# A transformer's opening laid out anew: the order of its first loads, silu of c from a broadcast load, own buffers for ten modulation loads

## The chip, the cores and the metric

The kernel runs on one core of a Trainium2 chip. The metric is the device time of one execution in microseconds (us); less is better. A core has TensorE (PE; its weight loads are listed as PEld), VectorE (DVE), ScalarE (ACT), GpSimd (POOL) and SyncE (SP), which issues all of this kernel's DMAs on one queue.

## The reference, cut to what matters

Two transformer blocks over 256 tokens of width 1024, in float32. The first block has two layers; each is modulated by a vector `c`:

```python
mod = jax.nn.silu(c) @ ada_w + ada_b
sh_m, sc_m, gt_m, sh_f, sc_f, gt_f = jnp.split(mod[:, None, :], 6, axis=-1)
h = rms_norm(x, norm_mix) * (1 + sc_m) + sh_m
(aq, ak, av, ..., cqkv, cz, ca, cb) = jnp.split(h @ w_in, points, axis=-1)
# window attention, sparse attention, gated delta rule -> o_a, o_b, o_c
x = x + gt_m * (jnp.concatenate([o_a, o_b, o_c], axis=-1) @ w_out)
h = rms_norm(x, norm_ffn) * (1 + sc_f) + sh_f
gate, up = jnp.split(h @ w_gate_up, 2, axis=-1)
x = x + gt_f * ((jax.nn.silu(gate) * up) @ w_down)
```

The second block has a cross attention to a memory `mem_2` of 256 rows of width 1024. Its keys and values are `rms_norm(mem_2, mem_norm_2) @ cross_wk_2` and `... @ cross_wv_2`. They depend on nothing else, and so they can be worked out first.

## The kernel before, in words

Features lie on the 128 partitions in eight blocks, tokens along the free axis. All weights are packed into one DRAM array in chunks of 128 rows by 1024 columns (512 KB; the token chunks `("win", l, "tok", i)` have 1104). A float32 product is made of three matmuls on parts: `weight` (L386) fetches a chunk into a `raw` buffer (L364; four of them), ACT copies it into a rounded high part `hi` (L393), VectorE subtracts to the low part `lo` (L394), and `mm3` (L425) multiplies hi by hi, hi by lo and lo by hi. The subtraction is the last reader of `raw`. A full chunk takes 24 matmuls for 256 tokens.

The modulation is not done on TensorE. `ada` (L668) fetches one column block of `ada_w` (512 KB) into a `side` buffer (four of them), and VectorE multiplies it by silu(c), which stands along the free axis of every partition (`crow`), and sums (L672). `ada_spread` (L410) sets how many columns are worked out beside each weight; `weight` counts that up and calls `ada` behind the split:

```python
        self.ada_due += self.ada_rate
        while self.ada_due >= 1 and self.ada_jobs:
            self.ada(*self.ada_jobs.pop(0))
            self.order(self.ada_last, d)
            self.ada_due -= 1
```

`order` fixes the order of two instructions of one engine, so that VectorE runs split, columns, next split. In the same way all loads are issued by SP in the order of the program (`load_last`, L364 and L649). Within what is fixed, a scheduler orders the instructions and gives buffers to tiles by a forecast of its own, at compile time; it adds a wait where a tile takes over a buffer.

The opening is `setup` (L633), `ada_spread` of 16 columns over `ADA0 = 11` weights and `mem_keys` (L1379), called in `run` (L1697). `setup` loads c as a column, the early column constants (`colt`: gains, biases), the memory in four loads (`mem_load`, L1368) and two constants (identity, ones). `mem_keys` then calls `c_row` (L660): 16 matmuls that turn silu(c) from a column into rows, and two copies out of PSUM. Next it scales the memory by its gain in two parts (`mem_parts`, L1374), and works out the memory's statistics: squares (ACT), sums (VectorE, PE), `rstd` (L441: VectorE, then a power on POOL), and `spread_sb` (L715: matmuls and a copy), which gives 1/rms along the free axis (`R`). Then come the keys: for each pair of eight weights wk0 to wk7 two times 24 matmuls (`ws`, L565) and a product with R into `memk` (L1398); behind the first and the second pair, two loads of x each. Then the values wv3 to wv7 (`mem_values`, L1402), with transposes.

In `run` the first layer follows: modulation bias (`ada_bias`), squares of x, `norm_hT` (L558), which for each of eight feature blocks makes a product on VectorE (L530), a high part on ACT (L535) and a low part on VectorE (L536), and `mixer` (L787). The mixer's steps are traced in the order of the string `SEQ[l]` (L271): `0` to `3` are heads of the delta rule, whose first step multiplies the chunk `("win", 0, ("qkv", 0), 0)`, `t` the token chunks (`tokens`, L797, `tok_steps`, L586). The chunks of layer 1's tokens are split ahead at the end of layer 0 (L1732).

Of the kernel before, what the change touches and what calls it, by code (L numbers as in the profile page):

```python
# [19 lines left out]
L = 2  # L20
# [5 lines left out]
CHUNK_COLS = 1104  # L26
# [27 lines left out]

def _plan():
# [3 lines left out]
    for l in range(L):  # L59
        for j in range(48):  # L60
            p["ada", l, j] = j
        for g, cols in WIN.items():
            for i, ks in enumerate(([0, 1, 2, 3], [4, 5, 6, 7]) if len(cols) > 128 else (K8,)):
                p["win", l, g, i] = [("w_in", l, ks, cols)]
# [154 lines left out]
def _pack(inputs):  # L219
# [26 lines left out]
    for l in range(L):  # L246
# [8 lines left out]
        "ccol": np.ascontiguousarray(i["c"].reshape(8, 128).T),  # L255
# [13 lines left out]
# the order in which the steps of a mixer are traced: 0..3 heads of the delta rule, i j inverses and x y outputs of its pairs,  # L269
# t tokens and decay, L loads, A modulation, c compress, r rope, m compressed, a window, b selected, z gate, p project, v memory values  # L270
SEQ = {0: "0tLttt0t001L11L1201i2ii22i3iiii32i3iAi3ii3jjjjcjijxcjjxjjcjjjxcxcjyycrcyrArrAAAyrrAArrmrabbAaaaabbbmbbbbAbbbzzAAzzAAzzApppAApApApAApAAAA",  # L271
       1: "vttvtv0vtt0001110211i2iiiiiii2333ii33iii2ixxxcc2jcjjjjjjjjjrjxcjjcjcrryrrrryyayacrrbmmbaAbaAAAbAbAzAbabAbzzbbbzzbzppppppp"}
HELD, HELD2 = 9, 8

# [6 lines left out]
def run(a):  # L281
    """traces a generator to its end and returns what that returns"""
    while True:
        try:
            next(a)
        except StopIteration as e:
            return e.value


def merge(a, b):  # L290
    """traces two generators in turns"""
    live = [a, b]
    while live:
        for g in list(live):
            if next(g, live) is live:
                live.remove(g)


class Net:
    def __init__(self, tc, ins, out):  # L300
# [6 lines left out]
        self.hold, self.held = (None, None), 0  # L307

# [55 lines left out]
    def fetch(self, key, tag="raw", bufs=4):  # L364
        off, n, _ = PLAN[key]
        cols = CHUNK_COLS if tag == "raw" else 1024
        raw = self.raw.tile([128, cols], F32, tag=tag, name=self.name("raw"), bufs=bufs)
# [8 lines left out]
    def order(self, later, earlier):  # L376
        """issue order of two instructions of one engine"""
# [3 lines left out]
    def ahead(self, keys):  # L381
        """weights that are loaded and split before they are asked for"""
        for k in keys:
            self.pre[k] = self.weight(k)

    def weight(self, key):  # L386
# [16 lines left out]
        self.ada_due += self.ada_rate  # L403
# [6 lines left out]
    def ada_spread(self, jobs, weights):  # L410
        """modulation columns to be worked out beside the next weights"""
# [3 lines left out]
    def pe(self, d):  # L415
        """keeps the tensor engine in the order of the trace while self.pe_order is set"""
# [29 lines left out]
    def row_rstd(self, halves, outs):  # L446
        """1 over the root mean square of the rows whose parts of 512 are given; outs are overwritten"""
# [18 lines left out]
    def to_hT(self, xn, scale, hi, lo, kcs):  # L466
        """xn: token tiles; hi(kc), lo(kc) [128, 256]: features on partitions, scaled, in two parts"""
# [12 lines left out]
    def square(self, b, gain=None, x=None):  # L480
        """feature blocks 2b and 2b+1 of (x * gain) ** 2, in addends of their sum"""
# [9 lines left out]
    def sums(self, sq, soon=False, after=None):  # L491
        """sums over features, tokens on partitions: PSUM [128, 2]"""
# [21 lines left out]
    def spread(self, r):  # L514
        """one value per token, along the free axis of all partitions: PSUM [128, 256]"""
# [10 lines left out]
    def norm_block(self, m, R, scale, shift, hi, lo):  # L526
        """x * scale * R (+ shift) in two parts, feature block m"""
# [10 lines left out]
    def scaled(self, m, scale, hi, lo, x=None):  # L538
        """x * scale in two parts, feature block m"""
# [5 lines left out]
    def new_hT(self, shift=None):  # L545
        """features on partitions, two parts; with shift, two more columns that hold it"""
# [6 lines left out]
    def pairs(self, n=4):  # L553
        """the same in pieces of two feature blocks"""
# [10 lines left out]
    def ws(self, keys, hT, turns=False, p=None):  # L565
        """features on partitions: [128, len(keys), 256] in one bank; turns: one feature block of hT after the other"""
# [19 lines left out]
    def tok_steps(self, keys, hT, outs):  # L586
        """tokens on partitions: outs[t] [128, n]; the chunks split the contraction"""
        n = 8 // len(keys)
        for i, key in enumerate(keys):
            wh, wl = (a.rearrange("p (k c) -> p k c", k=n) for a in self.weight(key))  # L590
            for t in range(2):
                ts = slice(t * 128, t * 128 + 128)
                for k in range(n):
                    kc = n * i + k
                    self.mm3(outs[t], (hT[0](kc)[:, ts], hT[1](kc)[:, ts]), (wh[:, k], wl[:, k]), kc == 0, kc == 7)
            yield
# [4 lines left out]
    def into(self, accs, m, l, w, first, last):  # L601
        """output features of block m: += w.T @ l; the two blocks of a bank form one accumulation group"""
# [13 lines left out]
    def project_steps(self, name, l, oT, accs, after=(), late=2, turn=range(8)):  # L616
        """1024 output features on partitions; the last contraction blocks finish one bank after the other"""
# [14 lines left out]
    # ------------------------------------------------------------------  # L632
    def setup(self):  # L633
# [7 lines left out]
        self.ccol = self.fix.tile([128, 8], F32, name="ccol")  # L641
        nc.vector.memset(self.mhalf, -0.5)
        self.loads([(self.ccol, ins["ccol"]), (self.colt[:, :COLS_EARLY], ins["cols"][:, :COLS_EARLY])])
        self.mem = self.mem_load()
        self.load_consts("ident", "one")
        nc.scalar.activation(self.ccol, self.ccol, AF.Silu)
# [13 lines left out]
    def c_row(self):  # L660
        """silu(c) along the free axis of all partitions"""
        for h in range(2):
            p = self.ps()
            for i in range(4):
                self.mm(p[:, i * 128:i * 128 + 128], self.ccol[:, 4 * h + i:4 * h + i + 1].to_broadcast([128, 128]), self.cc("ident"))
# [1153 lines left out]
```

## Time and profile before

| what | value |
|---|---|
| median of 3 runs | 1382.38 us |
| the three runs | 1381.71, 1382.38, 1386.05 us |
| span of the profiled execution, first to last instruction | 1381.5 us |
| mean granted TensorE clock of the profiled execution | 0.990 |
| PE, DVE, ACT, POOL busy, share of the span | 97%, 72%, 52%, 3% |
| moved by DMA | 276.71 MB, mean 200 GB/s |

The profile lists no other time of the profiled execution than its span; it lies 0.2 us under the fastest of the three runs. Busy time of PE is not PE at its peak, as its matmuls are pipelined and their ends are modelled. Where a line of the kernel is a helper (L393, L394, L423), the tile names tell the stages apart: `oT` holds the memory in two parts during the opening, `psw` is the bank that chunks accumulate into, `hhi` and `hlo` are the normed x.

### The profile page before, as it was taken

The page shows a single profiled execution, that of the slowest core. Times are in us where ns is not written, and L with a number is a line of the kernel's source. Part 1 is how long each engine was busy: PE and PEld are TensorE (multiplying, and loading weights), DVE is VectorE, ACT ScalarE, POOL GpSimd, SP SyncE. Part 2 cuts the span into 40 slices and gives each one's busy share as a digit, 9 for nine tenths or more (in the row PEclk, how much of TensorE's full clock was granted, in tenths as well). Part 3 has the DMA queues.
Part 4 walks back from the last instruction along what each step waited for, and adds up shares of the span by engine and source line. Part 5 has one row for each costly group of instructions (what it writes and reads, how often), then busy time and mean ns, then how long its engine had stood idle before and what let it go on. Part 6 is the DMA issues. An engine that isn't in the chain of part 4 may idle for free.

```text
span 1381.5 us, 26414 instructions
## 1 busy us (share of the span) xinstructions
PE 1341.2 (97%) x10632; PEld 1280.3 (93%) x10632; DVE 990.2 (72%) x1869; ACT 721.1 (52%) x1353; POOL 44.8 (3%) x55
## 2 busy tenths in 40 slices
PE   5899999999999999999999999999999999999998
PEld 5799879899999997889999999999987999999998
DVE  6888688998886886768666676665576664755554
ACT  4495274654445753666444454444456754644442
POOL 2001000000000010000000000000000000000000
PEclk9999999999999999999999999999999999999999
DMA  8974638899985445235666545555554563455551
GB/s 293 315 270 145 229 124 292 307 352 326 306 289 163 159 153 212 87 136 181 218 208 205 199 138 188 185 187 188 188 184 141 164 207 121 159 187 188 188 184 48
DMA packets 78747, 276.71 MB, mean 200 GB/s; under 512 B 9120, under 2 KB 9888, under 8 KB 78624
## 3 DMA queue, kind: packets, MB, share of 16 engines
q1 hardware_dynamic: 78624, 275.02, 58.7%
q8 instruction: 83, 1.36, 0.4%
q14 instruction: 40, 0.33, 0.1%
HBM read 271.31 MB, written 3.15 MB: 199 GB/s over the span
## 4 chain that ended last, share of the span: by engine, by line
PE 71%; issue 15%; DVE 7%; ACT 3%; DMA 2%; POOL 1%; SPq 0%; POOLq 0%; DVEq 0%; ACTq 0%
PE psw L423 41%; PE psb L423 22%; PE psi L423 5%; DVE lo L394 2%; PE psb L431 2%; DMA raw<-in_wbig_dram 1%; PE psb L1100 1%; ACT hi L393 1%; DVE raw L672 1%; POOL trs L444 1%; DVE hlo L543 1%; DVE xres L697 1%; POOL rr L943 1%; DMA xres<-in_x_dram 1%; DVE conv L921 0%
## 5 line engine op out<-in xcount | busy, mean ns | idle before, releaser
L394 DVE TENSOR_TENSOR lo<-raw,hi 128x1024 fp32r<-128x1024 f32 (+1 forms) x390 | 474.8, 1222 | 115.5 <-ACT hi L393 54.5
L423 PE MATMUL psw<-hhi,hi 128*128 128x256 f32 (+1 forms) x1744 | 496.6, 285 | 3.6 <-ACT hi L393 2.6
L423 PE MATMUL psw<-hhi,lo 128*128 128x256 f32 (+1 forms) x1744 | 494.9, 284 | 0.5 <-DVE lo L394 0.5
L423 PE MATMUL psw<-hlo,hi 128*128 128x256 f32 (+1 forms) x1744 | 495.1, 284 | 0.2 <-DVE hlo L543 0.2
L393 ACT ACTIVATE hi<-raw 128x1024 fp32r<-128x1024 f32 (+1 forms) x390 | 398.5, 1052 | 129.0 <-PE psw L423 66.4
L423 PEld LDWEIGHTS psw<-hhi,hi 128*128 128x128 f32 x1744 | 330.8, 190 | 5.9 <-ACT hi L393 3.2
L423 PEld LDWEIGHTS psw<-hlo,hi 128*128 128x128 f32 x1744 | 331.8, 190 | 1.6 <-issue 0.8
L423 PEld LDWEIGHTS psw<-hhi,lo 128*128 128x128 f32 x1744 | 331.8, 190 | 1.4 <-DVE lo L394 1.0
L423 PE MATMUL psb<-flo,hi 128*128 128x256 f32 x704 | 196.5, 281 | 0.0
L423 PE MATMUL psb<-fhi,lo 128*128 128x256 f32 x704 | 196.5, 281 | 0.0
L423 PE MATMUL psb<-fhi,hi 128*128 128x256 f32 x704 | 194.1, 281 | 0.2
L423 PEld LDWEIGHTS psb<-flo,hi 128*128 128x128 f32 x704 | 132.5, 188 | 0.2
L423 PEld LDWEIGHTS psb<-fhi,lo 128*128 128x128 f32 x704 | 132.5, 188 | 0.0
L423 PEld LDWEIGHTS psb<-fhi,hi 128*128 128x128 f32 x704 | 131.0, 188 | 1.0 <-ACT fhi L463 1.0
L672 DVE CUSTOM_DVE_ANT_0 raw<-raw,constt 128x1024 f32<-128x1024 f32 x96 | 116.0, 1218 | 0.0
L743 ACT ACTIVATE fa<-gu 128x256 f32<-128x256 f32 x44 | 18.4, 418 | 154.9 <-DVE gu L736 154.9
L423 PE MATMUL psb<-oT,hi 128*128 128x256 f32 x512 | 92.8, 283 | 0.0
L463 ACT ACTIVATE fhi<-fa 128x256 fp32r<-128x256 f32 x88 | 36.7, 418 | 97.6 <-DVE fa L741 54.9
L736 DVE TENSOR_TENSOR gu<-psw,R 128x512 f32<-128x512 f32 x44 | 30.4, 692 | 70.0 <-PE psw L423 66.5
L423 PEld LDWEIGHTS psb<-oT,hi 128*128 128x128 f32 x512 | 78.9, 188 | 0.3
L733 DVE TENSOR_TENSOR gu<-psw,R 128x256 f32<-128x256 f32 x88 | 37.0, 423 | 55.6 <-PE psw L423 53.6
L423 PE MATMUL psb<-oT,lo 128*128 128x256 f32 x256 | 71.8, 281 | 0.0
(368 smaller groups left out, 1753.9 us busy)
## 6 DMA issues: line engine op xcount, KB each, us to landing
raw<-in_wbig_dram SPq DMA_DIRECT2D x498, 512.0 KB, 4.4
raw<-in_wbig_dram SPq DMA_DIRECT2D x4, 552.0 KB, 5.6
mem<-in_mem_dram SPq DMA_DIRECT2D x8, 256.0 KB, 6.9
xres<-in_x_dram SPq DMA_DIRECT2D x4, 256.0 KB, 7.1
memd<-memk SPq DMA_DIRECT2D x4, 256.0 KB, 7.4
mk<-memd SPq DMA_DIRECT2D x4, 256.0 KB, 5.2
mv<-memd SPq DMA_DIRECT2D x2, 512.0 KB, 7.2
out_dram<-out SPq DMA_DIRECT2D x4, 256.0 KB, 2.4
```

The lines of the kernel that those rows point to most:

```text
L393: a = self.nc.scalar.activation(hi[:, :n], r, AF.Copy)
L394: d = self.nc.vector.tensor_tensor(lo[:, :n], r, hi[:, :n].bitcast(F32), op=OP.subtract)
L423: return self.pe(self.nc.tensor.matmul(out, lhsT, rhs, start=start, stop=stop))
L431: self.pe(self.nc.tensor.transpose(out, in_, self.cc("ident")))
L444: self.nc.gpsimd.tensor_tensor(dst, dst, self.mhalf[:, :n], op=OP.pow)
L463: self.nc.scalar.activation(hi, src, AF.Copy)
L543: self.nc.vector.scalar_tensor_tensor(lo(m), x, s, hi(m).bitcast(F32), op0=OP.mult, op1=OP.subtract))
L672: self.ada_last = self.nc.vector.tensor_tensor_reduce(w, w, self.crow, 1.0, 0.0, OP.mult, OP.add, m[:, j:j + 1])
L697: v.scalar_tensor_tensor(self.xk(m), a, gate[:, m:m + 1], self.xk(m), op0=OP.mult, op1=OP.add)
L733: nc.vector.tensor_tensor(s[:, i * 256:i * 256 + 256], p[i][:, :256], R, op=OP.mult)
L736: nc.vector.tensor_tensor(s.rearrange("p (a t) -> p a t", a=2), p.rearrange("p (a t) -> p a t", a=2), self.b3(R, 2), op=OP.mult)
L743: nc.scalar.activation(a, p[:, :256], AF.Silu)
```

## The change

- The opening's loads come in another order: the memory's gain by itself (4 KB, `memg`), the memory in two loads, wk0, wk1, c, the early column constants, identity and ones; then wk2 and the rest. x is loaded behind the second and third pair of weights, not behind the first and second.
- c is loaded along the free axis of all partitions with one broadcast load (128 times 4 KB), and one ACT instruction makes silu of it; `ccol`, the 16 matmuls and two copies go.
- wk0 and wk1 are fetched and split ahead of the pair's matmuls, and count no modulation columns: the 16 columns then lie beside the eleven weights wk2 to wv7.
- The first ten modulation loads have buffers of their own (`OWN = 10`), the rest share the four as before.
- The memory's statistics are traced behind the first pair's matmuls.
- The token chunks of both layers are three (3, 3 and 2 feature blocks; 828, 828 and 552 columns) instead of two of 1104, and the weight buffers are 1024 columns wide instead of 1104; one more `t` stands in each `SEQ`. What is split ahead for layer 1 stays two chunks.

```diff
-CHUNK_COLS = 1104
+CHUNK_COLS = 1024
...
+KCS = {"tok": ([0, 1, 2], [3, 4, 5], [6, 7]), True: ([0, 1, 2, 3], [4, 5, 6, 7]), False: (list(range(8)),)}
...
-            for i, ks in enumerate(([0, 1, 2, 3], [4, 5, 6, 7]) if len(cols) > 128 else (K8,)):
+            for i, ks in enumerate(KCS[g if g == "tok" else len(cols) > 128]):
...
-SEQ = {0: "0tLttt0t001L11L12...
+SEQ = {0: "0tLtttt0t001L11L12...
-       1: "vttvtv0vtt00011...
+       1: "vtttvtv0vtt00011...
+OWN = 10
...
     def fetch(self, key, tag="raw", bufs=4):
-        raw = self.raw.tile([128, cols], F32, tag=tag, name=self.name("raw"), bufs=bufs)
+        if tag == "side" and self.own:
+            self.own -= 1
+            raw = self.g4("own")
+        else:
+            raw = self.raw.tile([128, cols], F32, tag=tag, name=self.name("raw"), bufs=bufs)
...
-    def weight(self, key):
+    def weight(self, key, beside=True):
...
-        self.ada_due += self.ada_rate
+        self.ada_due += self.ada_rate if beside else 0
...
     def tok_steps(self, keys, hT, outs):
-        n = 8 // len(keys)
-        for i, key in enumerate(keys):
+        first = 0
+        for key in keys:
+            n = PLAN[key][1] // outs[0].shape[1]
...
-                    kc = n * i + k
+                    kc = first + k
...
     def setup(self):
-        self.ccol = self.fix.tile([128, 8], F32, name="ccol")
+        self.memg = self.fix.tile([128, 8], F32, name="memg")
         nc.vector.memset(self.mhalf, -0.5)
-        self.loads([(self.ccol, ins["ccol"]), (self.colt[:, :COLS_EARLY], ins["cols"][:, :COLS_EARLY])])
+        o, n = COLS.at["mem_norm_2"]
+        self.loads([(self.memg, ins["cols"][:, o:o + n])])
         self.mem = self.mem_load()
-        self.load_consts("ident", "one")
-        nc.scalar.activation(self.ccol, self.ccol, AF.Silu)
...
     def c_row(self):
-        for h in range(2):
-            p = self.ps()
-            for i in range(4):
-                self.mm(p[:, i * 128:i * 128 + 128], self.ccol[:, 4 * h + i:4 * h + i + 1].to_broadcast([128, 128]), self.cc("ident"))
-            self.nc.scalar.activation(self.crow[:, h * 512:h * 512 + 512], p, AF.Copy)
+        c = self.ins["c"]
+        self.loads([(self.crow, bass.AP(tensor=c.tensor, offset=c.offset, ap=[[0, 128], [1, D]]))])
+        self.nc.scalar.activation(self.crow, self.crow, AF.Silu)
...
     def mem_load(self):
-        mem = [self.c2("mem") for _ in range(4)]
-        for b in range(4):
-            self.loads([(mem[b].rearrange("p (a t) -> p a t", a=2), self.ins["mem"][:, 2 * b:2 * b + 2])])
+        mem = [self.g4("mem") for _ in range(2)]
+        for b in range(2):
+            self.loads([(mem[b].rearrange("p (a t) -> p a t", a=4), self.ins["mem"][:, 4 * b:4 * b + 4])])
...
     def mem_keys(self):
-        self.c_row()
+        self.pre["wk", 0] = self.weight(("wk", 0), False)
         for part in self.mem_parts(self.mem, mT):
             part()
-        r = self.token_rstd([s for b in range(4) for s in self.square(b, x=self.mem[b])])
-        self.memr = self.fix.tile([128, 2], F32, name="memr")
-        nc.vector.tensor_copy(self.memr, r)
-        R = self.spread_sb(r)
+        self.pre["wk", 1] = self.weight(("wk", 1), False)
+        self.c_row()
+        self.loads([(self.colt[:, :COLS_EARLY], self.ins["cols"][:, :COLS_EARLY])])
+        self.load_consts("ident", "one")
         for j in range(4):
             p = self.ws([("wk", 2 * j), ("wk", 2 * j + 1)], mT)
-            if j < 2:
-                self.loads([(self.x[:, 2 * b:2 * b + 2], self.ins["x"][:, 2 * b:2 * b + 2]) for b in (2 * j, 2 * j + 1)])
+            if j == 0:
+                r = self.token_rstd([s for b in range(4) for s in self.square(b, x=self.mem[b // 2][:, (b % 2) * 512:(b % 2) * 512 + 512])])
+                self.memr = self.fix.tile([128, 2], F32, name="memr")
+                nc.vector.tensor_copy(self.memr, r)
+                R = self.spread_sb(r)
+            if 1 <= j < 3:
+                self.loads([(self.x[:, 2 * b:2 * b + 2], self.ins["x"][:, 2 * b:2 * b + 2]) for b in (2 * j - 2, 2 * j - 1)])
```

## Rows read from the trace of the kernel before

**Rows 1.** The page: busy us (share of the span) xinstructions of each engine.

```profile
PE 1341.2 (97%) x10632; PEld 1280.3 (93%) x10632; DVE 990.2 (72%) x1869; ACT 721.1 (52%) x1353; POOL 44.8 (3%) x55
```

**Rows 2.** Table by stretches: length, busy us of PE/PEld/DVE/ACT/POOL, PE clock, DMA share, GB/s.

```profile
4.00:8.00 4.00, 0.00 (x0) 0.00 (x0) 0.88 (x2) 1.05 (x3) 3.58 (x10) 1.00 0.79 208
8.00:14.00 6.00, 3.83 (x17) 3.57 (x17) 4.80 (x10) 6.00 (x13) 0.00 (x0) 1.00 1.02 410
20.00:57.00 37.00, 30.72 (x243) 28.86 (x242) 30.89 (x46) 12.09 (x15) 1.62 (x1) 1.00 0.94 322
57.00:70.00 13.00, 10.39 (x80) 9.26 (x80) 10.45 (x23) 10.45 (x23) 0.00 (x0) 1.00 0.86 292
70.00:130.00 60.00, 59.32 (x468) 56.94 (x468) 50.29 (x123) 44.52 (x102) 4.23 (x4) 1.00 0.64 222
440.00:460.00 20.00, 18.02 (x124) 17.43 (x123) 15.96 (x33) 11.98 (x22) 1.55 (x1) 0.83 0.23 83
```

**Rows 3.** Waits, 0 to 70 us: us in total, times, longest.

```profile
ACT hi L393 <- DMA raw<-in_wbig_dram: 19.9, 9, 3.8
```

**Rows 4.** The chain that ended last, in order of time: start us, us, what.

```profile
0.73 0.39 SPq L651
...
2.58 5.90 DMA mem<-in_mem_dram
...
29.01 2.88 PE psw L423 x22
...
37.48 6.02 DMA raw<-in_wbig_dram
```

**Rows 5.** Timeline of VectorE: start us, us, instruction, idle time before it.

```profile
14.10 1.22 DVE L394 TENSOR_TENSOR lo<-raw,hi 128x1024 fp32r<-128x1024 f32 x1
...
24.31 1.22 DVE L394 TENSOR_TENSOR lo<-raw,hi 128x1024 fp32r<-128x1024 f32 x1
...
54.69 1.22 DVE L394 TENSOR_TENSOR lo<-raw,hi 128x1024 fp32r<-128x1024 f32 x1 [0.42 <-ACT hi L393]
55.83 1.22 DVE L672 CUSTOM_DVE_ANT_0 raw<-raw,constt 128x1024 f32<-128x1024 f32 x1
...
57.58 0.87 DVE L530 SCALAR_TENSOR_TENSOR hv<-xres,msc,psi 128x256 f32<-128x256 f32 x2
...
61.81 1.22 DVE L394 TENSOR_TENSOR lo<-raw,hi 128x1024 fp32r<-128x1024 f32 x1
```

**Rows 6.** Timeline of SyncE, its issues of weight loads: wk0, wk2, wk4.

```profile
4.01 4.17 SPq L369 DMA_DIRECT2D raw<-in_wbig_dram  x5
...
15.34 0.33 SPq L369 DMA_DIRECT2D raw<-in_wbig_dram  x1
...
25.56 0.33 SPq L369 DMA_DIRECT2D raw<-in_wbig_dram  x1
```

**Rows 7.** Waits of SyncE's queue, 0 to 70 us.

```profile
SPq L369 <- DVE mod L672: 12.2, 13, 1.9
```

**Rows 8.** Tile raw on SyncE: five loads issued 4 to 9 us, one at 25.6.

```profile
DMA to landing us min/median/max: 6.7/8.0/8.8
...
DMA to landing us min/median/max: 4.8/4.8/4.8
```

**Rows 9.** Timeline of PE: first matmuls of c's rows, of wk0, of the token chunk.

```profile
9.61 3.75 PE L423 MATMUL psb<-constt,ccol 128*128 128x128 f32 x16 [9.61 <-ACT oT L542]
...
13.92 0.38 PE L423 MATMUL psw<-oT,hi 128*128 128x256 f32 x1 [0.55 <-ACT hi L393]
...
72.51 0.29 PE L423 MATMUL psw<-hi,hhi 128*128 128x276 f32 x1
```

**Rows 10.** Timeline of ACT: six of the memory's scaled blocks, wk0's high part.

```profile
7.86 2.50 ACT L542 ACTIVATE oT<-mem,colt 128x256 fp32r<-128x256 f32 x6 [2.16 <-DMA mem<-in_mem_dram]
...
12.82 1.04 ACT L393 ACTIVATE hi<-raw 128x1024 fp32r<-128x1024 f32 x1
```

**Rows 11.** Tile row, 1000 to 1010 us: two broadcast loads of 256 KB.

```profile
DMA to landing us min/median/max: 5.0/5.1/5.2
```

More of the change, by code (lines that the diff above doesn't have):

```diff
@@ L254, in _pack @@
         "pos": np.ascontiguousarray(i["positions_2"][0].reshape(2, 128).T),
-        "ccol": np.ascontiguousarray(i["c"].reshape(8, 128).T),
         "c": np.ascontiguousarray(i["c"]),
@@ L268 @@
 PROJ = list(range(8))
-SEQ = {0: "0tLttt0t001L11L1201i2ii22i3iiii32i3iAi3ii3jjjjcjijxcjjxjjcjjjxcxcjyycrcyrArrAAAyrrAArrmrabbAaaaabbbmbbbbAbbbzzAAzzAAzzApppAApApApAApAAAA",
-       1: "vttvtv0vtt0001110211i2iiiiiii2333ii33iii2ixxxcc2jcjjjjjjjjjrjxcjjcjcrryrrrryyayacrrbmmbaAbaAAAbAbAzAbabAbzzbbbzzbzppppppp"}
+SEQ = {0: "0tLtttt0t001L11L1201i2ii22i3iiii32i3iAi3ii3jjjjcjijxcjjxjjcjjjxcxcjyycrcyrArrAAAyrrAArrmrabbAaaaabbbmbbbbAbbbzzAAzzAAzzApppAApApApAApAAAA",
+       1: "vtttvtv0vtt0001110211i2iiiiiii2333ii33iii2ixxxcc2jcjjjjjjjjjrjxcjjcjcrryrrrryyayacrrbmmbaAbaAAAbAbAzAbabAbzzbbbzzbzppppppp"}
 HELD, HELD2 = 9, 8
+OWN = 10
 def drain(a):
@@ L307, in __init__ @@
         self.hold, self.held = (None, None), 0
+        self.own = OWN
     def xk(self, m):
@@ L593, in tok_steps @@
                 for k in range(n):
-                    kc = n * i + k
+                    kc = first + k
                     self.mm3(outs[t], (hT[0](kc)[:, ts], hT[1](kc)[:, ts]), (wh[:, k], wl[:, k]), kc == 0, kc == 7)
+            first += n
             yield
@@ L798, in tokens @@
             ps = [self.pw() for _ in range(2)]
-            for _ in self.tok_steps([("win", l, "tok", i) for i in range(2)], hT, [q[:, :276] for q in ps]):
+            for _ in self.tok_steps([("win", l, "tok", i) for i in range(3)], hT, [q[:, :276] for q in ps]):
                 yield
@@ L1368, in mem_load @@
     def mem_load(self):
-        mem = [self.c2("mem") for _ in range(4)]
-        for b in range(4):
-            self.loads([(mem[b].rearrange("p (a t) -> p a t", a=2), self.ins["mem"][:, 2 * b:2 * b + 2])])
+        mem = [self.g4("mem") for _ in range(2)]
+        for b in range(2):
+            self.loads([(mem[b].rearrange("p (a t) -> p a t", a=4), self.ins["mem"][:, 4 * b:4 * b + 4])])
         return mem
     def mem_parts(self, mem, mT):
-        return [lambda m=m: self.scaled(m, self.pc("mem_norm_2"), *mT, x=mem[m // 2][:, (m % 2) * 256:(m % 2) * 256 + 256])[1]
+        return [lambda m=m: self.scaled(m, self.memg, *mT, x=mem[m // 4][:, (m % 4) * 256:(m % 4) * 256 + 256])[1]
                 for m in range(8)]
```

## The prediction, made before the change was run

> **What bounds the kernel now.** The page comes first: PE is busy for 97% of the span [rows 1]. The table by stretches then shows where the missing part lies: between 70 and 130 us PE works 59.3 of 60 us, while between 20 and 57 us it works 30.7 of 37, and before 8 us not at all [rows 2]. So the opening can be shortened, and what it gains is kept, since behind it a dense TensorE stretch merely starts earlier. The list of waits names what holds the opening: ACT waits 19.9 us in nine pieces for weights that are still on their way [rows 3]. The chain agrees: it goes through the memory's load, which lands at 8.48 us, and later through weight loads of 6 us, of which the one at 37.48 us stands here [rows 4]; there are two of them before 60 us.
>
> Why are weights late? Not because the DMA engines are full all the time: 410 GB/s flow from 8 to 14 us, but 322 from 20 to 57 us [rows 2]. The timeline of VectorE, beside the issues of the sync engine, shows the cause. The thirteen weights (wk0 to wk7, wv3 to wv7) and sixteen modulation columns alternate. The split of wk0 ends at 14.10 + 1.22 = 15.32 us and wk2 is issued at 15.34; the split of wk2 ends at 25.53 and wk4 is issued at 25.56 [rows 5, 6]. Of the four raw buffers two are in turn here, and a load waits until the last but one weight was split. In the same queue 13 loads wait for a modulation column to be read, 12.2 us in all [rows 7]. A load so issued lands 4.8 us later, or up to 8.8 us when many stand ahead [rows 8].
>
> The pace that follows: from wk2's split at 25.53 us to wv5's at 54.69 + 1.22 = 55.91 are eight weights, 3.80 us each [rows 5]. PE needs 2.88 us a weight [rows 4], VectorE 1.22 for the split and 16/11 x 1.22 for the columns, 3.0 us [rows 5]. Neither sets the pace; the round from a split over a load to the next split does.
>
> **The change, part by part.** All times are in the profiled execution (span 1381.5 us); the median of the three runs is 1382.4, so 0.9 is added at the end. My landmark is the end of the first q/k/v chunk, 72.51 us, where the first token matmul starts [rows 9]; from there PE is dense.
>
> *Start.* The two small loads, a constants load and two of the four memory issues leave the front of the queue: wk0's issue moves from 4.01 us [rows 6] to about 2.1: from 0.73 us on, a 4 KB gain and two memory blocks at some 0.4 us each, by the first issue's 0.39 [rows 4]. The memory is 1.05 MB. At 208 GB/s, the rate of 4 to 8 us, it needs 5.0 us; at 410 it needs 2.6 [rows 2]. I take the lower rate, which was measured on these same loads, and have it at 7 us; now the third of its four parts lands at 8.48 [rows 4]. Its eight scaled blocks then cost ACT about 0.42 us each (2.50 us for six) and wk0's split 1.06 us [rows 10]: PE starts on wk0 at about 10.5 us. Now its first matmul comes at 13.92 us [rows 9], and the statistics of the memory stand in between. These move behind wk1: all that they cost on ACT, VectorE and POOL now lies beside two weights' matmuls; were that cover gone, the first key product would wait, not PE.
>
> *silu of c.* Sixteen matmuls (3.75 us of PE from 9.61 us [rows 9]) and two evacuations go; they lay beside the loads and were worth nothing by themselves. In comes a 512 KB load. A broadcast read lands like any other: the two of 256 KB at 1001 us took 5.0 and 5.2 us [rows 11], as a weight does. Its price is one more transfer, 0.52 MB / 410 GB/s = 1.3 us, at 208 GB/s 2.5, paid by wk2 and all behind it. The activation, 1024 wide, costs what a split does, 1.06 us, for the two evacuations it removes; it delays wk2's split by nothing, as wk2 is in flight.
>
> *Second pair.* wk0's split ends at about 11.6 us. If wk2 still waits for it, it lands 4.8 us later, at 16.4, and its own split (1.06 + 1.22) could be done at 18.7; if it is issued ahead of that, at about 16. I take 17.5, against 25.53 now: 8 us won.
>
> *Pace.* Columns are worked out only beside wk2 to wv7, so eleven weights still carry sixteen. Ten of the sixteen get buffers of their own; their loads wait no more. If all that wait were on the path, 10/13 of 12.2 us over ten weights would be 0.9 us each, 3.80 - 0.94 = 2.9; but 2.6 loads a weight (columns, and x, counted in) at 410 GB/s need 3.4. If it is hidden, the pace stays 3.8. I take 3.6, the middle. The Trainium skill (DMA: Bandwidth & Descriptors, Where 436 GB/s comes from) says that for loads from HBM the HBM side binds at about 358 GB/s for a core; the 410 of rows 2 stand above that, so the measurement decides here. By that figure of the Trainium skill the 18.1 MB up to the last column could not land before about 53 us, which leaves my sum as it is and rules out the large gain below.
>
> *End of the opening.* wv7's split: 17.5 + 10 x 3.6 = 53.5 us, now 61.81 + 1.22 = 63.0. The last column is read right behind, at about 55; now it ends at 57.05, two weights earlier in the order. That is the price of the move: the norm of x then has no wv6 and wv7 beside it. Bias and scale take 0.5 us (57.05 to 57.58), each of eight blocks 0.44 us for its product (0.87 for two) and about as much for its low part, 7.1 in all, and two splits between them 2.4: 10 us [rows 5], so the last block at 65 and the q/k/v chunk, following block by block, at 65.4. Against 72.51: 7.1 us.
>
> *The rest.* The token chunk comes in three pieces instead of two; the elements that are split stay the same, and the fixed cost of one more split is below one split's 1.22 us [rows 5], beside dense PE. In layer 1 the third piece is no longer split ahead: 0 to +0.7 us (552 of 1024 columns of a split) in a stretch where PE waits for the norm, against 0 to -0.7 because the first piece needs three blocks, not four. I take 0. Ten buffers cost 40 KB per partition; smaller chunks give back 4.5. Whether later tiles must wait for them no row shows; they are read 20 us before the first mixer tile is wanted, so 0, at worst a few us.
>
> Sum: 1381.5 - 7.1 = 1374.4, by the median 1375.3 us. What is late next: the norm blocks on VectorE.
>
> **The rivals.** *No gain that counts:* the own buffers buy nothing and the uncovered norm costs more. The pace stays 3.8 and wk2 is done only at 18.7: last column at 58.2, landmark at 68.6; and PE, waiting for blocks, falls to 1.2 GHz as it does ahead of layer 1, where 440 to 460 us show 0.83 of the clock and 18.0 of 20 us busy [rows 2]: 17% of 20 us, or 3.4 us, are lost there. Then 1381.5 - 3.9 + 3.4 = 1381, 1382 by the median. For it: that same stage has no cover there. Against it: in 57 to 70 us the clock stays at 1.00. The Trainium skill (TensorE: Matmul & The Clock Gate, Part 1) says that an idle engine stands at 1.2 GHz; the 0.83 agrees, the full clock granted before the first matmul [rows 2] does not.
>
> *Much more:* the queue never runs dry. At 410 GB/s the 18.1 MB land by 2.3 + 44.2 = 46.5 us, PE needs 10.5 + 13 x 2.88 + 3 = 51; the last column at 51, landmark at 61.4: 1371.3. Against it: two raw buffers.
>
> *Slower:* the unblocked column loads stand ahead of the weights in the one queue, and a weight lands 8.0 us after its issue, as the early ones do [rows 8], not 4.8. With two buffers a pair then takes 8.0 + 1.06 + 1.22 = 10.3, 5.1 us a weight: last column at 17.5 + 51 + 1.2 = 69.7, landmark at 80, 1381.5 + 7.6, by the median 1390. It decides from a pace of 72.5 - 10.4 - 1.2 - 17.5 = 43.4 over ten, 4.3 us. Against it: at most two columns lie between two weights. That the buffers don't free the loads (the scheduler reuses addresses) would be the first rival again.
>
> **How the numbers follow.** Forecast 0.52 (1372.5 to 1378), no gain that counts 0.27 (1378.2 to 1384), much more 0.12 (1368 to 1372.5), slower 0.09 (up to 1390). A measurement of this kernel can tell 0.3%, 4.1 us, from no change: faster is below 1378.2, slower above 1386.5. So faster 0.64, same 0.28, slower 0.08. The range leaves out a little on both sides: 1369.5 to 1383.
>
> **What would show it.** Right: wk0's first matmul near 10.5 us; wk2's split done by 18; no wait of the queue on columns a0 to a9; 3.4 to 3.7 us a weight; the last column by 56 and the landmark by 67, with the same distance to the end as now (1309 us). Wrong: a pace of 3.8 or more, landings of 8 us in the middle, a clock below 1.00 around 60 us, or a distance behind the landmark that changes by over 2 us.

## The result, and the profile after

The change makes the kernel slower: 1395.01 us (median of four runs) against 1382.83 us, a ratio of 1.0093 with a 95% interval of 1.0070 to 1.0115. Forecast were 1375.3 us, faster. The profiled execution after took 1395.34 us, 1.7 us more than its span.

Engine totals and the stretches of [rows 2], in the kernel after (columns as there):

```profile
PE 1346.4 (97%) x10616; PEld 1285.0 (92%) x10616; DVE 995.8 (71%) x1871; ACT 730.2 (52%) x1356; POOL 45.2 (3%) x55
...
4.00:8.00 4.00, 0.00 (x0) 0.00 (x0) 0.99 (x3) 2.81 (x5) 3.58 (x10) 1.00 0.98 385
8.00:14.00 6.00, 3.94 (x16) 3.65 (x17) 4.72 (x9) 5.97 (x10) 0.00 (x0) 1.00 0.93 322
20.00:57.00 37.00, 30.13 (x210) 28.04 (x209) 28.08 (x44) 12.67 (x17) 3.14 (x2) 0.91 0.82 289
57.00:70.00 13.00, 11.26 (x76) 10.23 (x74) 8.33 (x16) 6.33 (x12) 0.00 (x0) 0.87 0.97 361
70.00:130.00 60.00, 54.81 (x406) 51.27 (x406) 47.42 (x116) 48.02 (x104) 3.33 (x4) 0.94 0.58 205
440.00:460.00 20.00, 17.85 (x141) 17.21 (x140) 13.61 (x26) 10.22 (x20) 1.55 (x1) 0.96 0.43 139
```

Compare the third and fifth with [rows 2]. Between 20 and 57 us PE runs 210 matmuls where it ran 243, and the granted clock, 1.00 before, is 0.91. Between 70 and 130 us, where PE had been dense, 5.2 us of the 60 are idle and the clock is 0.94.

SyncE's side of the kernel after: its four largest waits from 0 to 70 us (us in total, times, longest), then lines of its timeline between 4 and 60 us. A line that joins several issues is as long as they and the gaps between them.

```profile
SPq L377 <- DVE lo L402: 14.3, 3, 9.9
SPq L377 <- DVE mod L679: 13.0, 5, 7.0
SPq L377 <- PE psi L431: 10.0, 1, 10.0
SPq L377 <- ACT sq L492: 6.4, 1, 6.4
```

```profile
5.62 9.82 SPq L377 DMA_DIRECT2D own<-in_wbig_dram  x2
15.55 0.38 SPq L377 DMA_DIRECT2D raw<-in_wbig_dram  x1
...
31.52 0.49 SPq L377 DMA_DIRECT2D raw<-in_wbig_dram  x1
42.03 0.33 SPq L377 DMA_DIRECT2D own<-in_wbig_dram  x1
```

Twice the queue stands still ahead of a load into an "own" buffer, for a reader that has nothing to do with a column: column a1 goes out only at 15.12 us (the second half of the first line), column a8 at 42.03, 10 us behind the load before it. The first is let go by a square of ACT, the second by PE's `psi`, the matmuls that spread 1/rms of x. (The 7.0 us are a third stop, ahead of a12, which has no own buffer, until 52.2 us; the 9.9 us come behind the last column.) In [rows 7] the queue's longest wait for a column was 1.9 us.

The compiled programs give the reason. Addresses in bytes within a partition, kernel after, in the order of use:

```
mem, first half 53664   mem, second half 45472   x 45472
a0 49568   a1 53664   a2 37216   a3 53664   a4 37216   a5 41312
sums of x's squares 41312, 42336
a6 53664   a7 37216   a8 41312   a9 53664
```

Ten tiles of their own lie on four places. The trace holds no addresses, but it agrees: a4 goes out at 24.90 us, as a2, in the same place, has been read at 24.86; a6 at 29.95, behind a3 (29.92); a7 at 31.10, behind a4 (31.06). a1 takes the place of the memory, whose last readers are now the squares that the change moved back; a8 takes the place of the sums of x's squares, which live until x's statistics are done. (In the trace the matmuls that read these sums end at 39.30 us, and the queue is let go only by the spread, which ends at 41.96; why it waits for that later step is not shown.) In the kernel before, the three shared buffers lay apart, at 133984, 138080 and 142176; three of the four are in turn there, as a3 goes out at 16.55 us, when a0 has been read at 16.52.

Around and behind the second pause, in PE's and VectorE's timelines of the kernel after:

```profile
41.25 0.71 PE L431 MATMUL psi<-constt,trs 128*128 128x128 f32 x4 [1.61 <-POOL trs L452]
```

```profile
17.33 1.22 DVE L402 TENSOR_TENSOR lo<-raw,hi 128x1024 fp32r<-128x1024 f32 x1
...
45.79 1.23 DVE L679 CUSTOM_DVE_ANT_0 own<-own,constt 128x1024 f32<-128x1024 f32 x1 [1.72 <-DMA own<-in_wbig_dram]
...
63.80 1.23 DVE L402 TENSOR_TENSOR lo<-raw,hi 128x1024 fp32r<-128x1024 f32 x1 [0.52 <-ACT hi L401]
64.94 1.22 DVE L679 CUSTOM_DVE_ANT_0 raw<-raw,constt 128x1024 f32<-128x1024 f32 x1
...
66.62 1.66 DVE L538 SCALAR_TENSOR_TENSOR hv<-xres,msc,psi 128x256 f32<-128x256 f32 x4
```

`psi` runs from 41.25 to 41.96 us and a8 is issued at 42.03; wk2's split is done at 18.55 us (25.53 in [rows 5]), wv7's only at 65.03 (63.03 there): 4.65 us a weight. The last column is read at 66.16 us.

To see where the lead goes I counted, in each trace, the columns that PE's matmuls still have to stream. The table gives, for a time t of the kernel before, how much later (+) or earlier (-) another run has as much left, each in its one profiled execution; e1 to e9 are the experiments below.

```
t, us      25    35    45    65    80    250   440   1000  1370
after     -5.4  -5.8  +1.1  +2.3  +7.9  +9.9  +10.1 +11.5 +12.4
e1        -5.1  -5.7  -3.8  -3.1  +2.6  +3.0  +3.7  +3.3  +5.7
e5        -5.3  -6.1  -1.5  -3.0  +2.7  -3.3  -3.1  -6.3  -4.6
e9        -5.5  -5.8  -3.0  +1.0  +6.7  +0.7  +0.8  -2.3  -0.7
e4        -1.7  -0.4  -0.8  -0.7  -0.9  +0.2  +0.3  -0.5  +0.3
```

The start is won as forecast. The kernel after loses 7 us of it between 35 and 45 us, 5.6 us between 65 and 80 us, and more in and behind the first mixer.

The 10 us pause is not where the loss begins. Against e1, which has no own buffers, the kernel after is 4.5 us behind at 40 us (by e1's time), before a8 goes out; by then wk4 and wk5 have gone out 3.5 and 3.3 us later than there (at 20.95 and 25.32 us). At 54 us it is 2.6 us behind, at 60 us 5.1: wv6, which stands behind a12 in the queue, goes out at 54.23 us, 6.7 us later than in e1.

### The profile page after: what moved, and what is told of

It is laid out like the page before. It is cut to its first block, busy times and chain, and to the rows that moved or that the text cites. A ratio compares the mean times of both kernels' runs of the same rounds, so it can differ in the third digit from the quotient of the medians.

```text
span 1393.6 us, 26466 instructions
## 1 busy us (share of the span) xinstructions
PE 1346.4 (97%) x10616; PEld 1285.0 (92%) x10616; DVE 995.8 (71%) x1871; ACT 730.2 (52%) x1356; POOL 45.2 (3%) x55
## 4 chain that ended last, share of the span: by engine, by line
PE 46%; issue 14%; DVE 2%; ACT 1%; POOL 1%; DVEq 0%; POOLq 0%; ACTq 0%
PE psw L431 26%; PE psb L431 16%; PE psi L431 2%; PE psb L439 1%; PE psb L1107 1%; POOL trs L452 0%; DVE hlo L551 0%; DVE lo L402 0%; ACT hhi L550 0%; DVE xres L704 0%; ACT sq L496 0%; ACT sq L492 0%; DVE sb L1140 0%; POOL rr L950 0%; ACT hi L401 0%
## 5 line engine op out<-in xcount | busy, mean ns | idle before, releaser
L401 ACT ACTIVATE hi<-raw 128x1024 fp32r<-128x1024 f32 (+1 forms) x392 | 409.8, 1052 | 330.3 <-PE psw L431 175.7
L679 DVE CUSTOM_DVE_ANT_0 raw<-raw,constt 128x1024 f32<-128x1024 f32 x86 | 104.3, 1219 | 1.3 <-DMA raw<-in_wbig_dram 1.1
L431 PE MATMUL psw<-hi,hhi 128*128 128x256 f32 (+2 forms) x208 | 70.6, 343 | 2.5 <-ACT hi L401 2.5
L431 PE MATMUL psw<-lo,hhi 128*128 128x256 f32 (+2 forms) x208 | 69.3, 334 | 0.7 <-DVE lo L402 0.7
L431 PE MATMUL psw<-hi,hlo 128*128 128x256 f32 (+2 forms) x208 | 68.8, 334 | 0.0
```

Source lines behind the costliest of these rows:

```text
L401: a = self.nc.scalar.activation(hi[:, :n], r, AF.Copy)
L431: return self.pe(self.nc.tensor.matmul(out, lhsT, rhs, start=start, stop=stop))
L679: self.ada_last = self.nc.vector.tensor_tensor_reduce(w, w, self.crow, 1.0, 0.0, OP.mult, OP.add, m[:, j:j + 1])
```

## The experiments

Theory A: the queue's pauses, from shared addresses, make the loss. Theory B: the new order loses by itself. Theory C: the token chunks cost something behind the opening.

**e1, no own buffers**

```diff
-OWN = 10
+OWN = 0
```

> The changed kernel, but with no buffers of their own for the modulation columns: all sixteen go through the shared buffers, as before the change. Theory A (the loss sits in the one load queue: a column's own buffer takes over the address of the memory or of a square's sum, its load waits for the last reader of that, and all loads behind it wait too): both long pauses of the queue, 5.6 to 15.1 us and 32.0 to 42.0 us, go; the last column is read before 60 us (66.2 in the changed kernel), the first convolution starts by 74 (80.95), and the time is 1385 to 1389 us. Theory B (the new order of the opening loses by itself: columns and x stand ahead of weights, the norm stands uncovered, whatever the buffers): the first convolution stays at 79 to 82 us and the time at 1393 to 1397.

1389.39 us, ratio to the kernel before 1.0053 (1.0037 to 1.0069): 5.6 us less than after. The largest waits of the queue, 0 to 70 us, in this run:

```profile
SPq L377 <- DVE mod L679: 23.1, 12, 4.2
SPq L377 <- DVE lo L402: 15.8, 4, 8.0
SPq L660 <- ACT sq L492: 4.1, 1, 4.1
```

No wait for `psi` is left, and the first column loads go out at 5.70 and 6.27 us. (x still waits 4.1 us for the memory's squares, whose place it takes.) The last column is read at 62.54 us, not before 60. Theory A holds for its 5.6 us (its range is missed by 0.4 us), but 7 us remain that it doesn't explain.

**e2, truly own buffers**: slices of one tile.

```diff
-            raw = self.g4("own")
+            raw = self.ownt[:, (OWN - 1 - self.own) * 1024:(OWN - self.own) * 1024]
...
+            self.ownt = self.slot("ownt", OWN * 1024)
             self.mem_keys()
```

> The changed kernel, with the ten own buffers as slices of one tile of 40 KB, so that none shares an address with the memory, a square or another column while the opening runs. Theory A: no load of a column a0 to a9 waits for a reader; both long pauses go, the weights follow each other at 3.6 to 3.8 us, the last column is read by 57, the time is 1383 to 1388 us, a little under the kernel without own buffers. The prediction's own sum, if the buffers had been what it took them for: pace 3.6, last column at 55, first q/k/v chunk done at 65.4, and about 1375 plus what the token chunks cost. Theory B: as in the changed kernel, 1393 to 1397.

1391.86 us, 1.0072 (1.0057 to 1.0086): 2.5 us over e1, and in none of the expected ranges. A table by stretches of this run has one row worth keeping:

```profile
29.00:42.00 13.00, 10.00 (x69) 9.59 (x70) 12.34 (x20) 4.42 (x5) 1.56 (x1) 0.89 1.03 408
```

For 13 us the transfers run at 408 GB/s, and PE has its weights no sooner for it. The queue has run ahead, and its next column without an own buffer (a12, 42.0 to 49.9 us) stops it for 7.6 us in front of weights. (The Trainium skill, DMA: Bandwidth & Descriptors, Where 436 GB/s comes from, gives about 358 GB/s as what binds for a core's loads from HBM; this stretch stands above it, as the one in [rows 2] did.)

Nor is this queue free of strangers: x's loads wait 7.2 us for a sum of the memory's statistics.

**e3, own buffers in the kernel before**: the lines of `fetch` from the change's diff, and nothing else.

> The kernel before, with ten own buffers for the first ten columns and nothing else changed. Theory A: a buffer of its own is only a name: the ten lie on three addresses in turn, as the three shared buffers did, so the queue waits for a column's reader as often as before (13 times, 12 us) and the time is that of before, 1381 to 1385 us. The prediction's step (ten loads wait no more): the waits on columns a0 to a9 go and the last column comes 2 us earlier or more, 1381 or less. Theory B says nothing here.

1381.53 us, 0.9993 (0.9983 to 1.0003): nothing. The ten lie at 53664, 37216 and 41312 in turn there, as the three shared ones did.

**e4, token chunks in the kernel before**: `CHUNK_COLS`, `KCS`, `tok_steps` and `SEQ` from the change's diff.

> The kernel before, with the three smaller token chunks and the weight buffers of 1024 columns, and nothing else changed. Theory C (what the changed kernel loses behind the opening, some 2 us in the first mixer and 2 to 2.5 us in the rest, comes from the chunks): 1385 to 1388 us, the opening as before to within 0.5 us. Theory A with no C (the loss behind the opening is a consequence of the late start and the lower clock): 1381 to 1385 us.

1385.78 us, 1.0026 (1.0017 to 1.0036): theory C, 3.7 us. The executions of this kernel spread over 5 us; the profiled one, at 1383.48, is among the shortest, so the table above shows little of it.

**e5, the order alone**: e1 with the two token chunks, the 1104 columns and the `SEQ` of before.

> The changed kernel without own buffers and with the two token chunks of before: of the change only the new order of the opening is left. If the parts add up (own buffers 5.6 us, token chunks 3.7 us, both taken from the earlier runs), 1385 to 1387 us, 3 to 4 over the kernel before, and the first convolution starts at 75 to 77 us as in the run without own buffers. If the new order is worth the prediction's 7 us once the two other parts are gone: 1375 to 1378. If the parts don't add up: 1389 or more.

1378.47 us, 0.9981 (0.9971 to 0.9991): faster than before by 3.6 us, which lies in none of the expected ranges. With **e9** (e5 with the ten own buffers again) the square closes:

> The changed kernel with the ten own buffers, but with the two token chunks and the 1104-column buffers of before: it closes the square of own buffers and token chunks in the new order (with both 1395.0, without own buffers 1389.4, without both 1378.5). If the parts add up in the new order (own buffers 5.6, chunks 10.9): 1383 to 1386 us, with the two pauses of the load queue, 5.6 to 15.1 and 32 to 42 us, in place. If the chunks only cost something because the own buffers squeeze the memory: 1378 to 1380. If the own buffers alone make the whole loss: 1390 or more.

e9 took 1384.09 us, 1.0016 (1.0005 to 1.0028). Its queue has the same two stops, 6.4 us for a square and 7.6 us for `psi`.

```
medians, us, new order    no own buffers (e5, e1)   own buffers (e9, after)   own cost
two token chunks               1378.47                   1384.09               5.6
three token chunks             1389.39                   1395.01               5.6
chunks cost                      10.9                      10.9
```

The two parts add up (that they do so to the hundredth is luck: these are medians of several sessions, in which the kernel before had 1381.9 to 1382.8); but the chunks cost 10.9 us here and 3.7 in the old order. By the table of columns left, e1 and e5 are level at 80 us and 6.3 us apart at 250, of 10.3 us at 1370: the chunks act in the first mixer, and some 4 us behind it stay unexplained. The largest of PE's waits from 95 to 250 us, in the kernel before, in e5, in e1 and in e4:

```profile
PE psw L423 <- ACT hhi L542: 1.1, 1, 1.1
PE psb L423 <- DVE s L1218: 0.9, 1, 0.9
PE psb L423 <- DVE mx L1133: 0.4, 1, 0.4
```

```profile
PE psi L431 <- DVE Ec L992: 0.8, 1, 0.8
PE psb L431 <- DVE mx L1140: 0.2, 1, 0.2
```

```profile
PE psi L431 <- DVE Ec L1006: 1.3, 1, 1.3
PE psb L431 <- DVE mxb L1140: 0.9, 1, 0.9
PE psb L439 <- ACT braw L1166: 0.8, 1, 0.8
PE psb L439 <- DVE sa L1268: 0.5, 1, 0.5
```

```profile
PE psi L426 <- DVE Ec L1004: 1.3, 1, 1.3
PE psb L426 <- DVE mxb L1138: 0.9, 1, 0.9
PE psb L434 <- ACT braw L1164: 0.8, 1, 0.8
PE psb L434 <- DVE sa L1266: 0.5, 1, 0.5
```

e1 and e4 wait for the same things for the same time, though their openings differ. So I compared, from the first convolution to 250 us, the order of VectorE's instructions (360 to 400 of them):

```
order     runs                     in the same order as            PE, 80 to 250 us
first     before, e3               e3 with before: all                 0.0 (e3: by 300 us)
second    e1, e2, e4, e10, after   each with e1: all (e4: 385 of 386)  +0.4 to +2.0
third     e5, e9, e11, e13 to e15  each with e5: all                  -5.8 to -6.2
near 3rd  e7                       e7 with e5: some 370 of 398        -3.9
others    e6; e12; e8              e6 with e5: about half             +5.7; +0.6; -3.4
```

The last column is from the table of columns left (+ is time lost against the kernel before). In the three orders that runs share, the time in the mixer goes with the order whatever the opening was, and the change steps from the first order to the second. With two chunks it would have been the third. e7, below, has three chunks like e1, but nearly the third order, and -3.9 us: the time does not go with the number of chunks. No run changes that order alone, so this is a strict accompaniment and not a proof; the waits shown are its visible part, 3.5 us in e1 against 1.0 in e5. The rest is partly the clock, which is 0.98 from 130 to 200 us in e1 and 1.00 in e5.

**e10, three chunks with buffers of 1104 columns** (e1 with the old `CHUNK_COLS`):

> The new order without own buffers, with three token chunks but buffers of 1104 columns. Theory G (the order in which the scheduler puts the mixer behind three chunks costs, through waits of PE for VectorE between 100 and 240 us): 1386 to 1389 us, and PE waits there as in the run without own buffers (Ec, mxb, braw, sa, mx). Theory H (the width costs: with other addresses the scheduler has other buffers to wait for, and the slow drift from 640 to 1000 us comes with it): 1378 to 1381 us, no drift.

1388.17 us, 1.0052 (1.0031 to 1.0072): the loss comes with the third chunk, not with the width.

**e6, columns earlier**: e5 with `ADA0 = 9`.

> As the run of the opening's order alone, but the sixteen columns lie beside nine weights, wk2 to wv5, so that the last one is read two weights before the end, as in the kernel before. Theory D (what the new order loses is the norm of x, which stands behind the last column and has no weights beside it any more): the last column is read by 58 us, the first convolution starts by 73, the time is 1380 to 1383, 3 us or more under the run of the order alone. Rival (VectorE has more to do beside each weight, 1.78 columns instead of 1.45, and the weights come later by as much): the last split moves by as much as the last column gains, and the time is that of the order alone within 1.5 us.

1391.39 us, 1.0072 (1.0058 to 1.0086), and both theories have a part, though the last column (63.38 us) and the first convolution (78.14) miss theory D's times. From 66 to 76 us, in the kernel before, in e5 and in e6:

```profile
66.00:76.00 10.00, 8.97 (x70) 8.28 (x69) 8.80 (x13) 8.54 (x17) 0.00 (x0) 1.00 0.85 278
```

```profile
66.00:76.00 10.00, 6.08 (x30) 5.36 (x31) 8.92 (x15) 6.63 (x13) 0.00 (x0) 0.66 0.59 192
```

```profile
66.00:76.00 10.00, 8.56 (x67) 8.13 (x67) 8.93 (x17) 9.28 (x21) 0.00 (x0) 0.97 0.75 239
```

With the last column behind the last weight PE has 30 matmuls to do in the norm where it had 70, and then works at a granted clock of 0.50 to 0.58. Two weights behind the last column restore both. That is worth the 5.7 us that e5 loses between 65 and 80 us; but with 1.78 columns beside each weight the split of wv7 ends at 67.91 us instead of 61.44, and the mixer falls into another, slow order.

**e7 and e8, the columns on GpSimd's queue** (e8: from a3 on, in the kernel before)

```diff
+        on_pool = key[0] == "ada" and key[1] == 0 and key[2] < 16
-        d = self.nc.sync.dma_start(raw[:, :n], ...
+        d = (self.nc.gpsimd if on_pool else self.nc.sync).dma_start(raw[:, :n], ...
...
+        if on_pool:
+            if self.pool_last is not None:
+                self.order(d, self.pool_last)
+            self.pool_last = d
```

> The changed kernel without own buffers (three token chunks), with the sixteen column loads issued by GpSimd on a queue of its own, so that a column that waits for its buffer holds no weight. Theory E (the pace of 4.3 us a weight in the run without own buffers is the one queue's: weights stand behind columns that wait): the pace falls to 3.9 us or less, wv7's split ends by 58 us (61.4 there), and the time is 3 us or more under 1389.4. Rival F (the pace is set by VectorE, PE and the clock together, not by loads): pace 4.1 to 4.4, time 1387 to 1392. The first three columns now compete with the memory's load, which may cost up to 3 us at the start in both.

> The kernel before, with the columns from the fourth on issued by GpSimd on a queue of its own. Theory E: the 12.2 us for which the one queue waits for a column's reader no longer hold weights; but its weights waited mostly for the split two weights before (28.5 us), so the gain is at most 1 to 3 us: 1379 to 1382. Rival F: 1381 to 1384. If the second queue's transfers merely take bandwidth from the weights: 1384 or more.

e7: 1382.84 us, 1.0009 (0.9996 to 1.0022); its pace is 4.07 us, and wv7's split is done at 62.60 us, not earlier than in e1 (61.41), so theory E's 3.9 and 58 are missed. Its mixer, near the third order, takes 4.3 us less than e1's, and that is most of the 6.5 us. e8: 1381.98 us, 0.9999 (0.9987 to 1.0012), nothing. **e12**, the same with two chunks and three shared buffers:

> The opening's order alone (two chunks, no own buffers, three shared ones), with the sixteen column loads issued by GpSimd on a queue of its own. The run with three chunks gained 6.5 us by that queue (1389.4 to 1382.8). Theory E (weights held by columns in the one queue): the same gain here or half of it, 1372 to 1376 us, under both kernels. Rival (the gain came from another order of the mixer, not from the loads): 1377 to 1381.

1391.39 us, 1.0065 (1.0051 to 1.0079). The edit keeps GpSimd's loads in order too: one column's load waited 12.4 us for VectorE (the profile names `trs`, a step of the statistics; the reader of a column ends within 0.1 us of it), and the columns behind it waited with it, then the splits behind these columns. The second queue is no way out here, and theory E isn't shown.

**e11, e13 and e15, parts of the order undone in e5**: the statistics ahead of the first pair, x behind the first and second pair, both.

> The run of the opening's order alone (no own buffers, two chunks), with the memory's statistics traced ahead of the first pair's matmuls again. The prediction's step (moved behind wk1, the statistics lie beside two weights' matmuls and cost nothing): here PE starts the first pair 1 to 3 us later and the time is 1379.5 to 1382. Rival (the statistics stand in VectorE's way between wk2 and wk3 as well as between wk0 and wk1, so that nothing is gained by the move): 1377 to 1379.5.

> The opening's order alone (no own buffers, two chunks), with x loaded behind the first and second pair again, as before the change. VectorE and ACT run the first mixer in the same order as in the run of the opening's order alone, so that only the opening differs. If the late x holds the weights (its loads wait for the memory's squares and stop the queue): 1376 to 1378 us, the last column by 61. If the loads of x merely move the weights behind them: 1378.5 to 1381.

> As the run with x earlier, and with the memory's statistics ahead of the first pair too: of the opening's new order only the order of the first loads, silu from a broadcast load and the columns beside wk2 to wv7 are left. If neither move matters: within 1 us of the run with x earlier. If the memory's squares, done early, free the addresses that x waits for: 1 to 2 us under it.

e11: 1379.75 us, 0.9981 (0.9970 to 0.9992). e13: 1377.72, 0.9970 (0.9959 to 0.9982). e15: 1378.38, 0.9973 (0.9963 to 0.9984). All agree with e5 within their intervals: neither move makes a difference that these intervals, some 1.5 us to either side, can show (e11 lies on the border of its two ranges). The four are the fastest kernels of this study, 0.2 to 0.3% under the kernel before.

**e14, truly own buffers with two chunks** (e9 with the tile of e2):

> The changed kernel with ten truly own buffers (slices of one tile) and two chunks; the first mixer in the order of the run of the opening's order alone (1378.5). The prediction's step (own buffers bring the pace from 3.8 to 3.6 us a weight, the last column at 55): 1373 to 1376. Theory A as it stands after the run with three chunks, where true own buffers cost 2.5 us against none (the queue runs ahead, and its next column waits in front of weights): 1379.5 to 1382, pace 4.2 to 4.4.

1380.63 us, 0.9990 (0.9979 to 1.0000). The pace is 4.12 us a weight, e5's 4.29, and the time is no better than e5's, whose interval it overlaps. Real buffers for the ten columns did not bring the prediction's 3.6 either. But here, too, x's loads wait for a sum of the memory's statistics:

```profile
SPq L660 <- DVE sqs L507: 7.3, 1, 7.3
```

A queue in which no load waits for a stranger was not run.

## Why the prediction was wrong, step by step

*Start: right.* wk0's first matmul came at 9.60 us (10.5 forecast), wk2's split was done at 18.55 (17.5), and PE led by 5.4 us at 25.

*silu of c: nearly.* "It delays wk2's split by nothing" failed by 2.6 us. ACT's timeline in the kernel after:

```profile
11.71 1.28 ACT L673 ACT_TABLE_LOAD   x1
13.00 1.06 ACT L673 ACTIVATE constt<-constt 128x1024 f32<-128x1024 f32 x1
13.96 2.18 ACT L492 ACTIVATE sq<-mem 128x512 f32<-128x512 f32 x4
16.04 1.04 ACT L401 ACTIVATE hi<-raw 128x1024 fp32r<-128x1024 f32 x1
```

wk2 landed at 13.46 and waited for silu and the four squares. The table load in front I had not counted: 1.28 us. (The Trainium skill, ScalarE activation tables: per-element evaluation and per-set limits, What a function is on this engine, gives 1283 ns between two functions of different sets; the row agrees.)

The delay comes from silu and the squares together: silu ends 0.6 us behind the landing, and the squares, which the prediction laid "beside two weights' matmuls", stand behind it and take the other 2.0. (As an estimate from these rows, without the table load and silu, 2.3 us, the squares would have been done 0.3 us behind the landing.)

*Pace: this step failed first.* "Ten of the sixteen get buffers of their own; their loads wait no more." They waited more: 6.4 and 10.0 us at a stretch, for readers of other tiles. I had read a fresh name as fresh memory, and said of the addresses only that later tiles might wait, "so 0, at worst a few us"; it was the columns that waited. The pace was 4.65 us, not 3.6, and 5.6 us of the result are this. Behind it stands a second error: even without the pauses the new order runs at 4.1 to 4.3 us (e1, e5, e14), slower than the 3.75 of before. So the 3.6, "the middle", lay outside what any of these kernels did. This second error is the larger one. Of the 19.7 us between forecast and result, 15.0 lie ahead of the first convolution (80.95 us, 65.9 by the forecast) and 4.5 behind 80 us; in e5, without own buffers and with two chunks, the first convolution at 75.77 us still misses the forecast by 9.9, 7.6 of them by the last column.

*End of the opening: the term was too small.* I took 10 us from the last column to the end of the norm and 10.4 to the landmark. From the last column to the first convolution (0.5 us behind the landmark in the kernel before) it took 13.1 to 14.9 us in all runs of the new order on the one queue with `ADA0` of 11 (15.9 before, with two weights' matmuls in it), with PE at half clock for much of it. That loss I had put, at 3.4 us, into the rival and not into the sum.

*The rest: failed.* "I take 0" for the three chunks: they cost 3.7 us in the old order and 10.9 in the new. I had priced the splits that they add and not the order into which the scheduler puts the mixer. By the table, the distance from 80 us to the end grew by 4.5 us in the kernel after and shrank by 7.3 in e5; I had named a change over 2 us as a sign of error.

*The rivals.* The slower one had the right place, columns ahead of weights in the one queue, the right bound (a pace over 4.3) and a near landmark (80 us; measured some 80.5), the last by luck, as its pace of 5.1 was too slow and its end of 10.4 too short. It had not the trigger: not loads that no longer wait, but loads that wait for strangers. "That the buffers don't free the loads would be the first rival again", no gain, was wrong by 5.6 us. And the remark that a full clock was granted before the first matmul misread the rows, as the last section shows.

*The start's own worth.* Even e5 is 2.7 us behind at 80 us, and ahead only from the mixer on. The 6 us won at the start are given back to the pace and the uncovered norm; what e5 gains on the kernel before comes in the mixer, with the third order.

*Open.* Why the new order's pace is over 4 us is not settled: PE's low clock (0.91 from 20 to 57 us in e5, 1.00 before), the queue's waits for columns (24.3 us in twelve pieces in e5, 0 to 70 us) and the statistics go together in most runs, and moving x, the statistics or the queue did not part them. The clock alone is not it: in e14 it is 1.00 from 20 to 57 us, and the pace 4.12. Nor is a drift of 1 to 2 us between 600 and 1000 us in the kernel after, e1 and e4, where the clock lost the same as before. That a different order of the mixer alone changes the time was not tried.

## What to carry to other kernels

A tile with a name of its own is not a buffer of its own where a scheduler packs memory by lifetimes: look up the addresses, and ask of each load in an in-order queue whose last reader it waits for and what stands behind it. Moving a reader back (here the squares) lengthens the life of what it reads, and another load pays. And a small edit to what a compile-time scheduler sees is priced by the order that comes out, not by the instructions added: compare the instruction order of the stages that the edit does not touch, and measure the parts of a change apart.

## What the runs showed of the hardware

Behind waits PE may work at half its clock for some us. In the kernel after PE waits 1.17 and 0.75 us for wk5's parts between 31 and 35 us, and 1.61 us for `psi`'s input ahead of 41.25; these rows show the granted clock around that and around the norm:

```profile
34.00:39.00 5.00, 4.89 (x29) 4.89 (x29) 3.12 (x7) 1.88 (x3) 0.00 (x0) 0.66 0.85 345
42.00:45.00 3.00, 3.00 (x16) 3.00 (x16) 2.07 (x3) 0.00 (x0) 0.00 (x0) 0.50 0.64 187
...
72.00:80.00 8.00, 4.89 (x21) 4.08 (x22) 7.27 (x13) 4.85 (x10) 0.00 (x0) 0.57 0.25 72
```

From 42 to 45 us PE is busy all the time at a granted clock of 0.50, the 1.2 GHz level, and does 16 matmuls in 3 us; at 1.00 it does 28 (e1, 33 to 36 us). The clock fell behind several waits here; one of 1.61 us did not do it in e1, which has the same wait for `psi`'s input ahead of 37.94 us. So these 1.61 us are not the queue's doing either. Two rows of e1 (length, PE busy, clock, DMA share, GB/s), at the start and behind that wait:

```profile
12.00:15.00 3.00, 3.00 (x16) 1.00 1.02 419
...
39.00:42.00 3.00, 3.00 (x28) 1.00 0.83 281
```

The first shows that the clock's column can't be trusted at the start: PE is busy all the time and does 16 matmuls of the same form under a listed 1.00, as many as at 0.50. In the kernel after, the time from one matmul to the next halves at 14.4 us, and the trace's records of the granted clock begin only at 14.6. So the 1.00 of [rows 2] from 4 to 8 us shows no full clock.
